# Query weights into freed SBUF, the first head's queries by 128 tokens, the residual kept in SBUF, the last norm in quarters

## The chip, the cores and the metric

The kernel runs on one core of one Trainium2 chip. Each core has TensorE (PE in the profile; its weight loads are PEld), VectorE (DVE), ScalarE (ACT), GpSimd (POOL), the SyncE queue (SP) that only issues transfers here, and 16 DMA engines that all queues share. The metric is the device time of one execution in microseconds, the median over runs.

## The reference, cut to what matters

One layer works on 256 latent tokens and 256 context tokens with 2048 channels. Attention and a gated DeltaNet are computed from a common input projection, merged by gates and projected; the result is added to the stream. Then comes the expert stage, where each token picks 16 experts for each of 8 heads out of 128 x 128:

```python
x = x + g1 * y                                   # residual after the token mixer
hx = modulate(x, norm2_w, sh2, sc2)
q = (hx @ w_q).reshape(t, 8, 2, 128)             # two query halves for each head
s = einsum('thpd,pkd->thpk', q, sub_keys)        # 128 scores for each half
top_s, top_i = top_k(s, 16)                      # best 16 of each half, then the best 16 of 16x16 sums
idx = ...                                        # 128 expert rows for each token (8 heads x 16)
act = gelu(einsum('td,thkd->thk', hx, u[idx]))
x = x + g2 * einsum('thk,thkd->td', softmax(best_s) * act, v[idx])
return rmsnorm(x, final_norm_w)
```

`u` and `v` are tables of 16384 rows of 2048 fp32 numbers. 256 tokens with 128 experts each need 32768 rows of either table, 8 KB a row.

## The kernel before

Everything up to the output projection takes some 1190 us of the span. The output projection is a loop over 16 blocks of 128 channels (line 1190). Each block takes two loads of 512 KB of `wout`, rounded and split by ScalarE and VectorE into two parts for TensorE (`unit`, `split`, `mm3`), and two loads of 512 KB of `wmod` that VectorE reduces (`mod_unit`). The merged branches `mg_hi` and `mg_lo` (pool `mgp`, 32 KB a partition together) are the other operand. The updated residual `xl` has channels on the partitions; `keep_x1` (line 1179) transposes it by 128x128 blocks on TensorE, copies four blocks at a time out of PSUM, and stores them to DRAM (`x1_d`) on ScalarE's queue. After the loop, VectorE scales the 16 blocks of `mg` by the norm, and ScalarE adds the shift and writes `hx`, block by block (lines 1219 to 1221).

The expert stage handles the 256 tokens as two halves t of 128 (a token is a partition). `query(h)` (line 1447) forms the two query halves of a head, each as 16 products over a weight tile of 128x2048 (`wq`, 1 MiB) with 256 tokens as columns, copies them to SBUF and calls `scores`. A product in fp32 is two instructions in the trace. `route` is the ranking of one half of the tokens for one head: a row of small operations on VectorE that ends in 16 columns of row numbers. `first` gathers 128 rows of `u` with one column (GpSimd issues an indirect DMA of 1 MiB) and VectorE multiplies them with the token's `hx` and sums up, in one instruction. `hx_tokens` makes that `hx`, 16 transposes into PSUM. `second` gathers four times 128 rows of `v` and TensorE sums them up, in 32-token groups, with weights in `zw` into PSUM (`y`, four banks). Rows of 8 KB a partition, for weights and gathers alike, come from one pool of 14 buffers (`row()`); a request waits until its buffer is free.

The work is ordered by the planner of the language from the program's order and its estimates; `keep["on"]` and `keep_dve["on"]` fix the program's order on TensorE and VectorE from where they are set. Before, TensorE's order is fixed only from line 1489 on, VectorE's from line 1445. The order of the program is: the queries of head 0, its ranking for the first half, then for heads 1 to 4 the queries and the 16 gathers with the indices of the head before, with pieces of the next ranking between them; queries of heads 5 to 7; then four rounds of 16 steps, each with four gathers of `u` for the round after and four of `v`. Query weights 0 and 1 have tiles of their own (`wqa`), whose memory later becomes `zw`; 2 and 3 are asked for before head 0's queries, the others when their head comes up. `finish` adds the result to the residual and normalizes: the first half between the gathers of the third round, the second half after everything. It loads residual and norm weight through SP into rows.

## Time and profile before

| | |
|---|---|
| median of three runs | 2582.02 us (2573.47 to 2586.72) |
| the profiled execution's own time | 2578.54 us |
| its span, first to last instruction | 2576.8 us |
| granted TensorE clock, mean | 0.826 |
| busy: PE, DVE, ACT, POOL | 69%, 61%, 27%, 35% of the span |
| moved from and to HBM | 803.14 MB, 312 GB/s over the span |
| moved by the gathers' queue | 541.44 MB |

The durations below are from the one profiled execution. Times are counted from the span's start. A share of 1.00 in a DMA column says that all 16 engines were busy throughout. The share of a busy engine over the whole span mixes stages; here the expert stage, from 1190 us on, is looked at by itself.

### The profile page before, as it was taken

To read this page: it belongs to the slowest core of one execution; us is meant where nothing else is said; L and a number is where in the kernel's file an instruction comes from. 1 tells how busy PE (TensorE), PEld (TensorE's weight loads), DVE (VectorE), ACT (ScalarE), POOL (GpSimd) and SP (SyncE) were. 2 spreads that over 40 slices of the span, in tenths; PEclk is the share of its full clock that TensorE was granted. 3 is DMA by queue.
4 is the path that set the end of the run, shared out by engine and by line. 5 is a ranking of instruction groups with operands and counts; after the bars stand their busy time and mean duration, and the time that the engine had idled before them with its cause. 6 is when DMAs were issued, how large, how long until landed. Compare 5 with 4: busy or idle time off the path is not lost.

```text
span 2576.8 us, 28269 instructions
## 1 busy us (share of the span) xinstructions
PE 1774.1 (69%) x9908; PEld 1120.1 (43%) x9908; DVE 1580.3 (61%) x2769; ACT 696.4 (27%) x1627; POOL 890.0 (35%) x1108
## 2 busy tenths in 40 slices
PE   5899889888988999898343744554545445444664
PEld 2568777788888877788333500010000000000110
DVE  5237877778776588885898676656664454444001
ACT  3237656566655554343000100000000010000000
POOL 0000574747576000211423333333333333333331
PEclk7889999999999999999767876676776666766887
DMA  7755443455465588894999999999999999999995
GB/s 292 257 198 177 133 145 124 138 165 162 141 205 191 187 300 264 296 312 147 399 422 422 421 422 421 421 422 421 421 422 421 422 422 422 421 421 422 421 421 230
DMA packets 168526, 803.14 MB, mean 312 GB/s; under 512 B 26400, under 2 KB 45856, under 8 KB 99776
## 3 DMA queue, kind: packets, MB, share of 16 engines
q0 software_dynamic: 75296, 541.44, 50.7%
q1 hardware_dynamic: 76848, 250.58, 28.9%
q10 hardware_dynamic: 16240, 9.32, 1.2%
q8 instruction: 78, 1.28, 0.2%
q14 instruction: 64, 0.52, 0.1%
HBM read 788.94 MB, written 12.33 MB: 311 GB/s over the span
## 4 chain that ended last, share of the span: by engine, by line
DMA 44%; DVE 3%; PE 3%; issue 3%; POOL 1%; ACT 0%; POOLq 0%; ACTq 0%; DVEq 0%
DMA row<-in_u,ix 27%; DMA row<-in_v,ixT 17%; DVE row L181 2%; PE ps_mm L192 2%; POOL row L1257 1%; PE ps_y L192 0%; DVE sml L181 0%; PE ps_g L192 0%; DVE eq L181 0%; ACT row L1410 0%; DMA x_d<-xs 0%; DVE cf L181 0%; DVE bs L181 0%; PE ps_g L197 0%; PE ps_o L192 0%
## 5 line engine op out<-in xcount | busy, mean ns | idle before, releaser
L192 PE MATMUL ps_y<-row,zw 128*32 128x512 f32 x2048 | 572.6, 787 | 515.2 <-DMA row<-in_v,ixT 490.8
L181 DVE SCALAR_TENSOR_TENSOR row<-row,ps_h 128x2048 f32<-128x2048 f32 x256 | 582.1, 2281 | 427.1 <-DMA row<-in_u,ix 402.8
L192 PEld LDWEIGHTS ps_y<-row,zw 128*32 128x32 f32 x2048 | 98.1, 134 | 988.5 <-DMA row<-in_v,ixT 782.5
L1257 POOL DMA_INDIRECT row<-in_u,ix x256 | 240.6, 940 | 419.1 <-DMA row<-in_u,ix 256.3
L1257 POOL DMA_INDIRECT row<-in_v,ixT x256 | 241.2, 942 | 415.1 <-DMA row<-in_v,ixT 345.2
L181 DVE TENSOR_TENSOR lo<-raw,hi 128x512 fp32r<-128x512 f32 x408 | 303.9, 761 | 76.5 <-ACT hi L259 73.2
L192 PE MATMUL ps_mm<-h_hi,hi 128*128 128x256 f32 (+1 forms) x1040 | 342.1, 329 | 10.8 <-DVE gst L181 10.8
L192 PE MATMUL ps_mm<-h_hi,lo 128*128 128x256 f32 (+1 forms) x1040 | 323.4, 311 | 9.2 <-DVE lo L181 9.2
L192 PE MATMUL ps_mm<-h_lo,hi 128*128 128x256 f32 (+1 forms) x1040 | 323.4, 311 | 0.0
L259 ACT CAST hi<-raw 128x512 fp32r<-128x512 f32 x408 | 245.2, 618 | 196.1 <-PE ps_mm L192 123.3
L192 PEld LDWEIGHTS ps_mm<-h_hi,hi 128*128 128x128 f32 x1040 | 204.7, 197 | 31.8 <-DVE gst L181 11.8
L192 PEld LDWEIGHTS ps_mm<-h_hi,lo 128*128 128x128 f32 x1040 | 203.9, 196 | 20.0 <-DVE lo L181 10.3
L192 PEld LDWEIGHTS ps_mm<-h_lo,hi 128*128 128x128 f32 x1040 | 204.7, 197 | 9.3 <-issue 1.2
L821 POOL TENSOR_TENSOR qs<-qs,tq 32x30 f32<-32x30 f32 (+14 forms) x240 | 172.6, 719 | 18.7
L819 POOL TENSOR_TENSOR tq<-qs 32x30 f32<-32x30 f32 (+14 forms) x240 | 168.7, 703 | 18.1
L192 PE MATMUL ps_mm<-hx,row 128*128 128x256 f32 x448 | 108.4, 405 | 96.3 <-DMA row<-in_wq 96.3
L192 PEld LDWEIGHTS ps_mm<-hx,row 128*128 128x128 f32 x448 | 90.9, 205 | 110.6 <-DMA row<-in_wq 97.2
L1381 ACT ACTIVATE a<-a 128x64 f32<-128x64 f32 x4 | 1.0, 256 | 500.9 <-DVE row L181 500.9
L181 DVE TENSOR_TENSOR row<-ps_y,g2r 128x512 f32<-128x512 f32 x8 | 5.2, 678 | 176.0 <-PE ps_y L192 176.0
L1364 ACT ACTIVATE bs<-bs 128x64 f32<-128x64 f32 x4 | 1.0, 256 | 413.6 <-DVE bs L181 413.6
L181 DVE SCALAR_TENSOR_TENSOR mraw<-mraw,crow 128x1024 f32<-128x1024 f32 x73 | 92.9, 1275 | 16.9 <-DMA mraw<-in_wmod 16.5
L181 DVE SCALAR_TENSOR_TENSOR raw<-raw,crow 128x1024 f32<-128x1024 f32 x55 | 72.7, 1322 | 49.2 <-DMA raw<-in_wmod 49.1
(363 smaller groups left out, 2864.2 us busy)
## 6 DMA issues: line engine op xcount, KB each, us to landing
raw<-in_win SPq DMA_DIRECT2D x130, 512.0 KB, 4.4
raw<-in_wmod SPq DMA_DIRECT2D x119, 512.0 KB, 4.8
mraw<-in_wmod SPq DMA_DIRECT2D x73, 512.0 KB, 5.1
raw<-in_wout SPq DMA_DIRECT2D x32, 512.0 KB, 6.3
row<-in_wq SPq DMA_DIRECT2D x14, 1024.0 KB, 13.5
raw<-in_wbb SPq DMA_DIRECT2D x16, 512.0 KB, 5.8
raw<-in_wba SPq DMA_DIRECT2D x16, 512.0 KB, 4.6
wraw<-in_win SPq DMA_DIRECT2D x48, 128.0 KB, 4.8
```

Of the source, the lines that this page charges most:

```text
L181: ins = f(*a, **k)
L192: ins = nc.tensor.matmul(*a, **k)
L259: act.copy(hi, raw)
L819: pool.tensor_tensor(t, m[:, 0:s, s:s + 1].to_broadcast([32, s, w]), m[:, s:s + 1, s + 1:32].to_broadcast([32, s, w]), op=OP.mult)
L821: pool.tensor_tensor(m[:, 0:s, s + 1:32], m[:, 0:s, s + 1:32], t, op=OP.add)
L1257: pool.indirect_dma_start(out=r, out_offset=None, in_=I[table], in_offset=bass.IndirectOffsetOnAxis(ap=ix, axis=0))
L1364: act.activation(bs, bs, AF.Exp)
L1381: act.activation(a, a, AF.Gelu)
```

## The change

The pool of 14 rows becomes two pools of 4 and 9 rows. The 4 lie where `mg_hi` and `mg_lo` were; `row()` takes rows from the two pools in the order 4, 9, 4, 9. Query weights 0 to 3 are asked for into the 4 as soon as that memory is free, 4 to 7 when the larger pool opens, and 8 to 15 one after every eighth gather of heads 1 to 4. The queries of head 0 are formed for tokens 0 to 127 first, with their scores, then come the transposes of `hx_tokens`, then tokens 128 to 255; TensorE's order is fixed from there. The residual is copied from PSUM into an SBUF tile `x1s` and stays there (three blocks at the end of the loop, the last one by itself). The norm weight comes with the column constants and is spread over the partitions by 16 transposes, as the gate `g2r` is. `zw` has memory of its own. `y` is four tiles of one bank each. In `finish`, the product with the norm weight goes to a row of its own (`res`), so it does not overwrite the sum that ScalarE squares; the last scaling and the store go by quarters (0, 3, 1, 2; quarter 3 on ScalarE), and one small root operation is placed in the last round ahead of `finish`.

```diff
-    x1_d = dram.tile([2, 128, D], F32, name="x1_d")
...
     hx = hxp.tile([128, KB, T], F32, name="hx")
+    x1s = hxp.tile([128, 2, D], F32, name="x1s")
...
-    def keep_x1(i):
+    def keep_x1(i, n):
         for t in range(2):
             p = d_ps()
-            for j in range(4):
+            for j in range(n):
                 pe.transpose(p[:, j * 128:(j + 1) * 128], xl[:, i + j, t * 128:(t + 1) * 128], ident)
-            xs = b1.tile([128, 512], F32, name="xs", bufs=2)
-            act.copy(xs, p)
-            act.dma_start(x1_d[t, :, i * 128:(i + 4) * 128], xs)
-    ahead = []
+            act.copy(x1s[:, t, i * 128:(i + n) * 128], p[:, :n * 128])
...
         if i % 4 == 0 and i > 0:
-            keep_x1(i - 4)
-        if i in (11, 13):
-            w = hxp.tile([128, D], F32, name="wqa", tag="wz", bufs=2)
-            sp.dma_start(w, I["wq"][len(ahead)])
-            ahead.append(w)
+            keep_x1(i - 4, 4)
+        if i == 15:
+            keep_x1(12, 3)
...
-    keep_x1(12)
+    keep_x1(15, 1)
     dbg("hx", hx)
     st_mg.close()
+    rp, st_rp = open_pool("rp", side=R)
+    ROWS_R, ROWS_L = 4, 9
+    rows = {"n": 0}
+    def row():
+        i = rows["n"] % (ROWS_R + ROWS_L)
+        rows["n"] += 1
+        p, n = (rp, ROWS_R) if i < ROWS_R else (ex, ROWS_L)
+        return p.tile([128, D], F32, name="row", bufs=n)
+    def wq_load(i):
+        r = row()
+        sp.dma_start(r, I["wq"][i])
+        return r
+    ahead = [wq_load(i) for i in range(4)]
...
-    ROWS = 14
-    def row():
-        return ex.tile([128, D], F32, name="row", bufs=ROWS)
...
-    ahead += [wq_load(i) for i in range(2, 4)]
+    loaded = {"n": 8}
+    ahead += [wq_load(i) for i in range(4, 8)]
...
+    fwr = ex.tile([128, D], F32, name="fwr")
+    zw = [ex.tile([128, 4, 512], F32, name="zw%d" % i) for i in range(2)]
+    for z in zw:
+        pool.memset(z, 0.0)
...
+    def scores(h, q, t, p):
+        for hf in range(2):
+            pe.matmul(p[:, t * T + hf * 128:t * T + (hf + 1) * 128], q[hf][:, t * 128:(t + 1) * 128],
+                      subk[:, hf], start=True, stop=True)
+        if t == 0 and h < 4:
+            s = ex.tile([128, T], F32, name="s", bufs=2)
+        else:
+            s = sc[:, h - 4 if t == 0 else 4 + h]
+        act.copy(s, p[:, t * T:(t + 1) * T])
+        return s
...
-                pe.matmul(y[32 * g:32 * g + 32, cs], zw[f][:, g, 32 * b:32 * b + 32], rows[g][:, cs],
+                pe.matmul(y[c][32 * g:32 * g + 32, :], zw[f][:, g, 32 * b:32 * b + 32], rows[g][:, cs],
...
-        tmp, x, fw = row(), row(), row()
-        sp.dma_start(x, x1_d[t])
-        sp.dma_start(fw, I["fnw"].to_broadcast([128, D]))
+        tmp, res = row(), row()
+        x = x1s[:, t]
         f = fs[:, t]
         cs = [slice(c * 512, (c + 1) * 512) for c in range(4)]
         if t == 0:
-            for c in cs:
-                dve.tensor_tensor(tmp[:, c], y[:, c], g2r[:, c], op=OP.mult)
+            for i, c in enumerate(cs):
+                dve.tensor_tensor(tmp[:, c], y[i], g2r[:, c], op=OP.mult)
             yield
         for i, c in enumerate(cs):
             if t == 1:
-                dve.tensor_tensor(tmp[:, c], y[:, c], g2r[:, c], op=OP.mult)
+                dve.tensor_tensor(tmp[:, c], y[i], g2r[:, c], op=OP.mult)
             dve.tensor_tensor(x[:, c], x[:, c], tmp[:, c], op=OP.add)
             act.activation(tmp[:, c], x[:, c], AF.Square, accum_out=f[:, i:i + 1])
-            dve.tensor_tensor(x[:, c], x[:, c], fw[:, c], op=OP.mult)
+            dve.tensor_tensor(res[:, c], x[:, c], fwr[:, c], op=OP.mult)
             yield
         dve.tensor_reduce(f[:, 4:5], f[:, 0:4], axis=AX.X, op=OP.add)
         dve.tensor_scalar(f[:, 4:5], f[:, 4:5], 1.0 / D, EPS, op0=OP.mult, op1=OP.add)
...
         dve.tensor_scalar(f[:, 7:8], f[:, 7:8], -0.5, 1.5, op0=OP.mult, op1=OP.add)
         dve.tensor_tensor(f[:, 6:7], f[:, 6:7], f[:, 7:8], op=OP.mult)
         yield
-        for c in range(2):
-            xs = x[:, c * 1024:(c + 1) * 1024]
-            if c == 0:
-                act.activation(xs, xs, AF.Copy, scale=f[:, 6:7])
+        for i in (0, 3, 1, 2):
+            if i == 3:
+                act.activation(res[:, cs[i]], res[:, cs[i]], AF.Copy, scale=f[:, 6:7])
             else:
-                dve.tensor_scalar(xs, xs, f[:, 6:7], None, op0=OP.mult)
-            sp.dma_start(out[t * 128:(t + 1) * 128, c * 1024:(c + 1) * 1024], xs)
+                dve.tensor_scalar(res[:, cs[i]], res[:, cs[i]], f[:, 6:7], None, op0=OP.mult)
+            sp.dma_start(out[t * 128:(t + 1) * 128, cs[i]], res[:, cs[i]])
...
+    def query(h, parts):
+        ws = [ahead.pop(0) for _ in range(2)]
+        os_ = [psm("mm") for _ in range(2)]
+        q = [ex.tile([128, T], F32, name="q", bufs=4) for _ in range(2)]
+        p = psm("g")
+        for a, z in parts:
+            for j in range(2):
+                for k in range(KB):
+                    pe.matmul(os_[j][:, a:z], ws[j][:, k * 128:(k + 1) * 128], hx[:, k, a:z],
+                              start=k == 0, stop=k == KB - 1)
+                act.copy(q[j][:, a:z], os_[j][:, a:z])
+            for t in range(a // 128, z // 128):
+                S[h, t] = scores(h, q, t, p)
+            if a == 0 and z == 128:
+                yield
+    def first_queries():
+        g = query(0, ((0, 128), (128, 256)))
+        next(g)
+        o = hx_tokens(0)
+        all_of(g)
+        return o
+    S = {}
+    keep["on"] = True
+    h_ = first_queries()
+    all_of(route(0, 0, S[0, 0]))
     for h in range(1, NH):
-        query(h)
+        all_of(query(h, ((0, 256),)))
         if h < 5:
-            work.append(route(0, h, S[h][0]))
+            work.append(route(0, h, S[h, 0]))
             for c in range(h * 16 - 16, h * 16):
                 first(0, c, h_)
                 if c % 16 > 2:
                     piece()
+                if c % 8 == 7:
+                    ahead.append(wq_load(loaded["n"]))
+                    loaded["n"] += 1
...
-        if h == 2:
-            zw = [hxp.tile([128, D], F32, name="zw%d" % i, tag="wz", bufs=2).rearrange("p (g c) -> p g c", g=4)
-                  for i in range(2)]
-            for z in zw:
-                pool.memset(z, 0.0)
-    for i in range(0, 16, 4):
-        p = psm("g")
-        for j in range(4):
-            pe.transpose(p[:, j * 128:(j + 1) * 128], modc[:, 80 + i + j:81 + i + j].to_broadcast([128, 128]), ident)
-        act.copy(g2r[:, i * 128:(i + 4) * 128], p)
+    for dst, src in ((g2r, modc[:, 80:96]), (fwr, cols[:, C_FN:C_FN + 16])):
+        for i in range(0, 16, 4):
+            p = psm("g")
+            for j in range(4):
+                pe.transpose(p[:, j * 128:(j + 1) * 128], src[:, i + j:i + j + 1].to_broadcast([128, 128]), ident)
+            act.copy(dst[:, i * 128:(i + 4) * 128], p)
...
-        return psy.tile([128, D], F32, name="ps_y", tag="y", bufs=1)
+        return [psy.tile([128, 512], F32, name="ps_y%d" % c, tag="y%d" % c, bufs=1) for c in range(4)]
...
+            if n == 3 and b == 1:
+                tc.keep_in_program_order(act.activation(fs[:, 1, 5:6], epsc, AF.Sqrt))
```

## Rows read from the trace of the kernel before

**Rows 1.** Windows: PE, PEld, DVE, ACT, POOL busy us, clock, DMA share, GB/s.
```profile
1232.00:1420.00 188.00, 69.30 (x280) 58.08 (x280) 174.55 (x269) 9.41 (x31) 60.56 (x66) 0.69 1.01 422
1420.00:2540.00 1120.00, 598.19 (x2172) 128.87 (x2172) 540.90 (x806) 43.71 (x151) 415.69 (x442) 0.72 1.01 421
```

**Rows 2.** Chain that ended last, one link of the long stretch: start, us.
```profile
2266.33 19.13 DMA row<-in_v,ixT
2285.49 0.72 issue
```

**Rows 3.** Windows between the last projection weights and the first gather.
```profile
1184.00:1192.00 8.00, 7.96 (x66) 7.55 (x64) 1.62 (x3) 1.32 (x3) 0.00 (x0) 1.00 0.01 2
...
1215.00:1220.00 5.00, 5.00 (x29) 4.51 (x28) 4.62 (x21) 0.36 (x1) 0.00 (x0) 1.00 0.01 3
```

**Rows 4.** DMA issues with KB and median us to landing; line 1263's landings.
```profile
row<-in_wq SPq DMA_DIRECT2D x14, 1024.0 KB, 13.5
...
row<-x_d SPq DMA_DIRECT2D x2, 1024.0 KB, 8.9
...
DMA to landing us min/median/max: 5.3/13.5/21.8
```

**Rows 5.** Timeline of SP's queue: start, us from first to last issue.
```profile
1203.19 188.47 SPq L1263 DMA_DIRECT2D row<-in_wq  x14
...
1238.51 2.82 SPq L1263 DMA_DIRECT2D row<-in_wq  x2
...
2522.24 0.33 SPq L1398 DMA_DIRECT2D row<-x_d  x1
```

**Rows 6.** Timeline of VectorE: the last product of the output projection is used.
```profile
1191.56 0.48 DVE L181 SCALAR_TENSOR_TENSOR xl<-ps_mm,modc,xl 128x256 f32<-128x256 f32 x1 [5.73 <-PE ps_mm L192]
```

**Rows 7.** Timelines and chain (PE) from hx to the first gathered row.
```profile
1196.62 6.50 ACT L1221 ACTIVATE hx<-mg,modc 128x256 f32<-128x256 f32 x16 [1.95 <-DMA x_d<-xs]
...
1197.18 15.65 PE ps_mm L192 x64
...
1214.28 0.29 DVE L181 MAX8 sml<-s 128x8 f32<-128x128 f32 x1 [12.66 <-ACT s L1291]
...
1223.76 0.17 DVE L181 CAST ix<-ef 128x16 uint32<-128x16 f32 x1
...
1224.89 1.02 POOL L1257 DMA_INDIRECT row<-in_u,ix  x1 [10.19 <-DVE ix L181]
...
1231.02 2.29 DVE L181 SCALAR_TENSOR_TENSOR row<-row,ps_h 128x2048 f32<-128x2048 f32 x1 [7.09 <-DMA row<-in_u,ix]
```

**Rows 8.** Timeline of TensorE: transposes of 128 columns, and the next product.
```profile
1214.79 1.15 PE L197 MATMUL ps_h<-ck,hx 128*128 128x128 f32 x9
1215.77 6.42 PE L192 MATMUL ps_mm<-hx,row 128*128 128x256 f32 x29
```

**Rows 9.** VectorE's groups by form, 1225 to 1422 us: busy, mean ns, idle before.
```profile
L181 DVE SCALAR_TENSOR_TENSOR row<-row,ps_h 128x2048 f32<-128x2048 f32 x65 | 146.4, 2279 | 18.2 <-DMA row<-in_u,ix 17.7 <-issue 0.3
```

**Rows 10.** Waits of TensorE, 1085 to 1192 us: total, times, longest.
```profile
PE ps_mm L192 <- ACT hi L259: 5.6, 6, 1.7
```

**Rows 11.** Timelines of PE, DVE, ACT and SP after the last row; issues.
```profile
2552.43 5.12 PE L192 MATMUL ps_y<-row,zw 128*32 128x512 f32 x26 [1.43 <-DMA row<-in_v,ixT]
...
2557.59 0.69 DVE L181 TENSOR_TENSOR row<-ps_y,g2r 128x512 f32<-128x512 f32 x1 [175.98 <-PE ps_y L192]
...
2559.84 0.69 DVE L181 TENSOR_TENSOR row<-row 128x512 f32<-128x512 f32 x1 [0.84 <-ACT row L1410]
...
2568.24 1.28 ACT L1415 ACT_TABLE_LOAD   x1
...
2570.74 1.15 ACT L1425 ACTIVATE row<-row,fs 128x1024 f32<-128x1024 f32 x1 [1.00 <-DVE fs L181]
...
2571.52 0.81 SPq L1428 DMA_DIRECT2D out<-row  x2
...
out<-row SPq DMA_DIRECT2D x2, 512.0 KB, 3.1
```

More of the change, by code (lines that the diff above doesn't have):

```diff
@@ L30 @@
 CHUNKS = tuple((k, k + 2) for k in range(0, 16, 2))
-C_BMOD, C_N1, C_N2, C_QN, C_KVN, C_CONV, C_DNW, C_ALOG, C_DTB = 0, 96, 112, 128, 132, 134, 254, 255, 256
-N_COL = 257
+C_BMOD, C_N1, C_N2, C_QN, C_KVN, C_CONV, C_DNW, C_ALOG, C_DTB, C_FN = 0, 96, 112, 128, 132, 134, 254, 255, 256, 257
+N_COL = 273
 K_ID, K_IOTA, K_I16, K_PERSIST = 0, 128, 256, 272
@@ L140, in layout @@
     cols[64:80, C_DTB] = dn_dt_bias[0].reshape(16)
+    cols[:, C_FN:C_FN + 16] = final_norm_w.reshape(16, 128).T
     a["cols"] = cols
@@ L162, in layout @@
     a["v"] = np.ascontiguousarray(peer_v[0])
-    a["fnw"] = np.ascontiguousarray(final_norm_w.reshape(1, D))
     a["ck"], a["ca"] = shape_constants()
@@ L1259, in gather @@
         return r
-    def wq_load(i):
-        r = row()
-        sp.dma_start(r, I["wq"][i])
-        return r
-    ahead += [wq_load(i) for i in range(2, 4)]
+    loaded = {"n": 8}
+    ahead += [wq_load(i) for i in range(4, 8)]
     subk = ex.tile([128, 2, 128], F32, name="subk")
@@ L1278, in tile_block @@
                     (("bs", F32), ("ef", F32), ("ix", U32), ("ixT", U32), ("a", F32))})
-    def scores(h, q):
-        p = psm("g")
-        out_ = []
-        for t in range(2):
-            for hf in range(2):
-                pe.matmul(p[:, t * T + hf * 128:t * T + (hf + 1) * 128], q[hf][:, t * 128:(t + 1) * 128],
-                          subk[:, hf], start=True, stop=True)
-            if t == 0 and h < 4:
-                s = ex.tile([128, T], F32, name="s", bufs=2)
-            else:
-                s = sc[:, h - 4 if t == 0 else 4 + h]
-            act.copy(s, p[:, t * T:(t + 1) * T])
-            out_.append(s)
-        return out_
+    def scores(h, q, t, p):
[8 more added lines that the diff above has]
+        return s
     def route(t, h, s):
@@ L1441, in all_of @@
             pass
-    S = []
     keep_dve["on"] = True
-    def query(h):
-        qs = []
-        for j in range(2):
-            o = psm("mm")
-            w = ahead.pop(0) if ahead else wq_load(2 * h + j)
-            for k in range(KB):
-                pe.matmul(o[:, :T], w[:, k * 128:(k + 1) * 128], hx[:, k], start=k == 0, stop=k == KB - 1)
-            q = ex.tile([128, T], F32, name="q", bufs=4)
-            act.copy(q, o[:, :T])
-            qs.append(q)
-        S.append(scores(h, qs))
-    query(0)
-    all_of(route(0, 0, S[0][0]))
-    h_ = hx_tokens(0)
+    def query(h, parts):
[23 more added lines that the diff above has]
+    all_of(route(0, 0, S[0, 0]))
     for h in range(1, NH):
-        query(h)
+        all_of(query(h, ((0, 256),)))
         if h < 5:
-            work.append(route(0, h, S[h][0]))
+            work.append(route(0, h, S[h, 0]))
             for c in range(h * 16 - 16, h * 16):
@@ L1469, in tile_block @@
                     piece()
+                if c % 8 == 7:
+                    ahead.append(wq_load(loaded["n"]))
+                    loaded["n"] += 1
             while work:
                 piece()
-        if h == 2:
-            zw = [hxp.tile([128, D], F32, name="zw%d" % i, tag="wz", bufs=2).rearrange("p (g c) -> p g c", g=4)
-                  for i in range(2)]
-            for z in zw:
-                pool.memset(z, 0.0)
-    for i in range(0, 16, 4):
-        p = psm("g")
-        for j in range(4):
-            pe.transpose(p[:, j * 128:(j + 1) * 128], modc[:, 80 + i + j:81 + i + j].to_broadcast([128, 128]), ident)
-        act.copy(g2r[:, i * 128:(i + 4) * 128], p)
+    for dst, src in ((g2r, modc[:, 80:96]), (fwr, cols[:, C_FN:C_FN + 16])):
[4 more added lines that the diff above has]
+            act.copy(dst[:, i * 128:(i + 4) * 128], p)
     st_psb.close()
@@ L1485, in y_tile @@
     def y_tile():
-        return psy.tile([128, D], F32, name="ps_y", tag="y", bufs=1)
-    keep["on"] = True
+        return [psy.tile([128, 512], F32, name="ps_y%d" % c, tag="y%d" % c, bufs=1) for c in range(4)]
     y = [y_tile(), None]
@@ L1493, in tile_block @@
         if n == 0:
-            work += [route(0, h, S[h][0]) for h in range(5, 8)] + [route(1, h, S[h][1]) for h in range(4)]
+            work += [route(0, h, S[h, 0]) for h in range(5, 8)] + [route(1, h, S[h, 1]) for h in range(4)]
         if n == 1:
-            work += [route(1, h, S[h][1]) for h in range(4, 8)]
+            work += [route(1, h, S[h, 1]) for h in range(4, 8)]
         for b in range(16):
@@ L1518, in tile_block @@
     st_ex.close()
+    st_rp.close()
     st_hx.close()
```

## Prediction

> **What bounds the kernel now.** I read the windows first, then the chain of waits, then the queue's own views. From 1232 us to 2540 us of the span the 16 DMA engines are busy to a share of 1.01 at 421 to 422 GB/s, while TensorE, ScalarE and GpSimd are well under full throughout, and VectorE in all but the first 188 us [rows 1]. The chain says the same: a gather of 1 MiB waits 19.13 us for its data, 0.72 us pass, and the next link follows [rows 2]. A 1 MiB transfer at 421 GB/s takes 1.0486 MB / 421 GB/s = 2.49 us, so 19.85 us is eight transfers: eight gathers are in flight, and the queue stays full. In this stage only three things count: how many MiB pass, when the stream starts, and what follows its last byte. In those first 188 us VectorE is nearly as full (174.55 us busy) [rows 1]; this matters below.
>
> Around the stream are two idle places. Before it, between the last output-projection weights and the first gather, the engines are at 0.01 (1184 to 1192 us) and again at 0.01 (1215 to 1220 us) [rows 3]. After it, the last row wakes TensorE at 2552.43 us and the span ends at 2576.8 us: 24.4 us in which little more than two output stores moves.
>
> **Bytes that leave the stream.** Fourteen loads of query weights (1024 KB each), two reloads of the residual and, by the same pattern, two of the norm weight pass through SP's queue [rows 4]. The first two of the fourteen leave at 1203.19 us; the third and fourth only at 1238.51 us [rows 5], and the other ten later still, so 12 lie in the full stretch. The residual and norm loads lie there too; the second pair leaves at 2522.24 us, among the last gathers [rows 5]. That is 16 MiB beside 512 gathers. After the change four loads (0 to 3) go into the memory of the merged branches, free when the last output-projection product is done, about 1191.5 us [rows 6], and four (4 to 7) when the scaled residual is no longer read, about 1203 us. The quickest of these loads landed 5.3 us after its issue [rows 4]; with 2.49 us for each further one the first four land by 1191.5 + 5.3 + 3 x 2.49 = 1204.3 us and the next four by 1216 us: both inside the valley of [rows 3]. Loads 8 to 15 stay in the stream; the other four vanish. So 16 - 8 = 8 transfers, 8 x 2.49 = **19.9 us**.
>
> The rule of the Trainium skill that bears on this is in "DMA: Bandwidth & Descriptors", section "Issuing engines are not separate DMA queues": transfers from all issuing engines run on the same 16 engines and interleave. By it a load asked for earlier wins nothing where the engines are full; the trace agrees with the premise, as gathers and weight loads together never pass 422 GB/s [rows 1]. This is the third rival below.
>
> **The stream starts earlier.** Now the first head's products take 15.65 us for 64 instructions of 256 columns, 0.245 us each, and then VectorE ranks from 1214.28 us and the first gather leaves at 1224.89 us, 10.6 us behind [rows 7]. With 128 columns the first product (32 instructions) is paced by ScalarE, which delivers the 16 blocks of hx in 6.50 us from 1196.62 us [rows 7], so it ends near 1203.3 us. The second takes 32 x 0.122 = 3.9 us if half the columns cost half: 1207.2 us instead of 1212.8 us. Gain 5.6 us; first gather at 1219.3 us. No row shows this product at 128 columns. The nearest do: nine 128x128 instructions, each with a weight load of its own, start at 1214.79 us, and the next product at 1215.77 us, 0.109 us each [rows 8]. Bounds: 0 us gained (128 columns cost as much as 256) and 5.6 us; I take the latter. The first load must be there by 1199.4 us (1203.3 less 3.9); it lands at 1191.5 + 5.3 = 1196.8 us. If the four loads share the engines and land together at 1204.3 us, 7.8 us of products start only then, and all but 0.7 us of the gain is gone.
>
> The Trainium skill, "TensorE: Matmul & The Clock Gate", section "Back-to-back issue gap", speaks against halving: it gives about 81 ns per product at 128 columns and 131 ns at 512, so a quarter of the columns costs 0.62. An estimate on that line has half of 256 columns at about 0.83; the second product would take 6.5 us and the sum would be 2.6 us smaller. The 0.109 us of [rows 8] go by columns, so the sum does too.
>
> **What the other parts cost.** The second half of the first head (7.8 us) and sixteen transposes (16 x 0.109 = 1.7 us [rows 8]) now stand between the first scores and the second head on TensorE. The second head's scores come about 5 us later than now (1236 instead of 1231 us), and VectorE, in program order, needs them after four rows: about 1 us of waiting, which the queued gathers cover. Rows: 14 become 13, and at the start 8 of the 13 hold weights. Five gathers go at once, four of the held rows come free as the first two heads' products end, to about 1235 us, and used rows come back from 1228 us on. I followed row by row who frees what, with the durations above and VectorE's 2.28 us a row [rows 9]: the first 16 gathers and two weight loads keep the engines full to about 1267 us, the next head's indices are there near 1261 us, and the queue runs dry for about 1.5 us near 1403 us and some 3 us where the first half's last norm holds two rows. Against the 5.6 us I set **5 us** lost; bounds 0 and the 14 us of the second rival. VectorE's own work for the first 64 rows is 146.4 us (65 of them) [rows 9] and four rankings at the 9.65 us that the first one takes (1214.28 to 1223.93 us) [rows 7], 185 us in all: from the first row in use at 1225.4 us to 1410 us. The 64 gathers and 8 weight loads need 72 x 2.49 = 179 us from 1223 us, to 1402 us, and eight gathers in flight bridge the 8 us between the two, so neither holds the other up.
>
> Keeping the residual in SBUF replaces a store by nothing: the copies out of PSUM stay. Filling the norm weight's tile costs 16 more transposes (16 x 0.109 us) and four copies out of PSUM behind the last queries, some 4 us beside a full DMA queue, which covers it: nothing. If that cover is gone, 4 us.
>
> **Before the stream** six residual stores of 128x512 elements (1.5 MiB) and one weight load leave the output-projection stage. TensorE waits there 5.6 us for weights that ScalarE rounds as they land [rows 10]; the 5.6 us are the most that fewer bytes can give back, and nothing the least. I take **3 us**, the middle.
>
> **After the last row.** Now 5.12 us of products end, then VectorE starts (2557.59 us), and in each quarter the multiplication by the norm weight waits 0.84 us for ScalarE's square, because it overwrites what the square reads [rows 11]. Four quarters last to 2568.24 us, where a table load of 1.28 us lies in the way of the root; the halves are scaled from 2570.74 us (1.15 us) and stored from 2571.52 us, 0.4 us an issue and 3.1 us a store, the last landed near 2575.0 us [rows 11]. After: each quarter has its own PSUM tile, so the first starts when 2 of the 26 products are done, 0.6 us behind the last row. VectorE then needs 3 x 0.69 = 2.07 us a quarter without the wait, 8.3 us: TensorE's 5.12 us run beneath, and the last square is done at about 9.1 us. From there to the scale it is 2.5 us now (2568.24 to 2570.74); without the table load, but with some 0.6 us of summing that ran beneath it, 1.8 us: 10.9 us. The first quarter is scaled by 11.3 us; four stores issued 0.4 us apart end at 12.5 us, the last lands at 15.2 us if half the bytes take a little less than 3.1 us, and 1.8 us remain to the end of the span as now: 17.0 us instead of 24.4 us, **7.4 us**. If a quarter is stored as slowly as a half, 7.0 us; if twice as fast, 8.2 us.
>
> **Sum**: 19.9 + 5.6 - 5 + 3 + 7.4 = 30.9 us. The profiled execution took 2578.5 us (span 2576.8 us), 3.5 us under the median of the three runs, so 2547.6 us on its footing and **2551 us** as a median. What a measurement can tell from no change is about 0.5%, 12.9 us.
>
> **Rivals.** (1) *Some row count decides, slower.* With 13 rows instead of 14 the gathers may wait for rows in the long stream, not only at its start. A gather alone takes 1231.02 - 1224.89 = 6.1 us from issue to use [rows 7], 2.5 transfers; only with two or fewer in flight do the engines idle, 6.1 / 2 - 2.49 = 0.57 us a gather. 55 such gathers eat the 31 us, all 512 would cost 290 us. Against it: eight are in flight [rows 2], so 13 rows leave 5 for use before the queue even thins. A case of a hundred such gathers gives 2607 us. (2) *Rows in strict turn.* If the ninth gather must have the row of weight load 4, it waits for the third head's first product, and three more wait for the next ones, 7.8 us apart where the engines need 2.49 us. That idles them about 17 us, of which 14 are lost: 17 us gained, 2565 us. Nothing in the rows shows which row a gather gets. (3) *The early loads do not land in the valley*, or VectorE holds the first stage and the weights' share of the bytes is not given back: then only the four residual and norm loads count, 10 us less, 21 us gained, 2561 us. For it: VectorE's 174.55 of 188 us [rows 1]. (4) *Not told from no change*: both (2) and (3), 30.9 - 14 - 10 = 7 us gained, 2575 us.
>
> **Chances.** Forecast 0.62 (2543 to 2559 us, by the 0 to 5.6 us of the start, 0 to 5.6 us of the stage before and 3 us for rows), rival 2 0.13, rival 3 0.13, rival 4 0.08, rival 1 0.04. The range 2541 to 2567 us holds the forecast, most of rivals 2 and 3, and no more than 2 in 10 is left out. Faster by over 0.5% is below 2569 us: the first three but a little, 0.86; within 0.5% 0.10; slower 0.04.
>
> **What would show it.** Right: four weight loads leaving near 1191.5 us and four near 1203 us; the first gather near 1219 us; no residual or norm load in the stream; a full DMA share from about 1223 us and the last row some 20 us earlier than 2552.4 us less what the earlier stage gives; VectorE's last quarter about 8 us behind the last row. Wrong: DMA share under 0.95 between 1240 and 1280 us with GpSimd waiting for a query product (rival 2); ranking that begins where it does now; fewer than eight gathers in flight in the long stretch (rival 1). What would make the number wrong most easily is a first weight load later than 1199 us, or a planner's order of the copies on ScalarE that holds up the query products.

## The result, and the profile after

| | before | after |
|---|---|---|
| median of four executions | 2580.75 us | 2540.32 us |
| lowest and highest | 2573.47, 2586.72 us | 2534.12, 2543.52 us |
| span of the profiled execution | 2576.8 us | 2541.8 us |
| ratio after / before | | 0.9842, 95% interval 0.9809 to 0.9875 |

The changed kernel is 1.6% faster, 40.4 us by the medians. The prediction said 2551 us within 2541 to 2567 us: the time lies 0.7 us below that range. Three of the five terms came out near their size and one on the good side of it; the cost set against them was too small, and one term was missing.

Windows of the stream after (columns as in [rows 1], which they answer):

```profile
1232.00:1420.00 188.00, 114.45 (x458) 95.26 (x456) 177.34 (x278) 15.55 (x47) 62.85 (x67) 0.77 0.99 414
1420.00:2060.00 640.00, 319.89 (x1066) 56.39 (x1066) 389.28 (x655) 30.55 (x112) 245.80 (x259) 0.71 1.01 427
2060.00:2110.00 50.00, 23.59 (x68) 4.12 (x72) 25.43 (x34) 6.38 (x12) 13.76 (x15) 0.62 0.81 322
2110.00:2500.00 390.00, 220.41 (x861) 40.53 (x854) 119.84 (x106) 5.19 (x19) 150.29 (x160) 0.76 1.01 427
```

Two things here were not forecast. The long stretches run at 427 GB/s at the same DMA share of 1.01 where [rows 1] had 421. And there is a hole at 2060 to 2110 us, with a smaller one in the first 188 us.

The start after, timelines of SP, ScalarE, TensorE, VectorE and GpSimd ([rows 5, 7]):

```profile
1191.37 2.09 SPq L1232 DMA_DIRECT2D row<-in_wq  x4
1203.12 1.99 SPq L1232 DMA_DIRECT2D row<-in_wq  x4
1196.56 6.49 ACT L1216 ACTIVATE hx<-mg,modc 128x256 f32<-128x256 f32 x16 [1.95 <-DVE mg L181]
1197.12 10.04 PE L192 MATMUL ps_mm<-hx,row 128*128 128x128 f32 x64 [3.47 <-ACT hx L1216]
1209.01 0.68 PE L192 MATMUL ps_g<-subk,q 128*128 128x128 f32 x4 [1.84 <-DMA subk<-in_subk]
1211.27 7.31 PE L192 MATMUL ps_mm<-hx,row 128*128 128x128 f32 x64
1210.54 0.30 DVE L181 MAX8 sml<-s 128x8 f32<-128x128 f32 x1 [8.98 <-ACT s L1295]
1220.48 1.02 POOL L1264 DMA_INDIRECT row<-in_u,ix  x1 [13.76 <-DVE ix L181]
```

Both groups of weight loads leave when forecast. The first products are done at 1207.2 us, as forecast, and 64 instructions of 128 columns take 7.31 us (0.114 us each; [rows 7] had 0.245 us at 256). But the scores then wait for `subk`, the sub-keys. Their load is asked for only at 1203.08 us, with the second four weight loads, when the memory of its tile is free; it takes 5.5 us to land.

The tail after, timelines of TensorE, VectorE, ScalarE and SP, and one line of DMA issues ([rows 11]):

```profile
2524.21 3.62 PE L192 MATMUL ps_y<-row,zw 128*32 128x512 f32 x26 [1.41 <-DMA row<-in_v,ixT]
2525.30 0.69 DVE L181 TENSOR_TENSOR row<-ps_y,g2r 128x512 f32<-128x512 f32 x1 [164.88 <-PE ps_y L192]
2526.75 0.69 DVE L181 TENSOR_TENSOR row<-x1s,fwr 128x512 f32<-128x512 f32 x1
2532.91 0.63 ACT L1412 ACTIVATE row<-x1s 128x512 f32<-128x512 f32 x1 [1.33 <-DVE x1s L181]
2534.11 0.20 ACT L1417 ACTIVATE fs<-fs 128x1 f32<-128x1 f32 x1 [0.47 <-DVE fs L181]
2535.31 1.28 DVE L181 TENSOR_SCALAR row<-row,fs 128x512 f32<-128x512 f32 x3
2535.82 1.80 SPq L1429 DMA_DIRECT2D out<-row  x4
out<-row SPq DMA_DIRECT2D x8, 256.0 KB, 3.3
```

VectorE starts 1.1 us behind the last row, the product with the norm weight waits for nothing, and no table load stands before the root: 17.6 us from the last row to the end instead of 24.4 us.

### The profile page after: what moved, and what is told of

Read it like the earlier page. It is cut to its first block, busy times and chain, and to the rows that moved or that the text cites. A ratio compares the mean times of both kernels' runs of the same rounds, so it can differ in the third digit from the quotient of the medians.

```text
span 2541.8 us, 28426 instructions
## 1 busy us (share of the span) xinstructions
PE 1788.7 (70%) x9988; PEld 1132.7 (45%) x9988; DVE 1581.1 (62%) x2773; ACT 699.6 (28%) x1636; POOL 901.2 (35%) x1108
## 4 chain that ended last, share of the span: by engine, by line
DMA 54%; PE 20%; DVE 8%; issue 7%; POOL 6%; ACT 4%; another core or an unknown queue 0%; SPq 0%; DVEq 0%; ACTq 0%; POOLq 0%
DMA row<-in_v,ixT 39%; PE ps_mm L192 12%; PE ps_d L192 4%; DMA row<-in_u,ix 3%; DMA raw<-in_wout 3%; POOL qs L820 3%; POOL tq L818 2%; PE ps_r L192 2%; DMA raw<-in_wmod 2%; DVE lo L181 2%; DMA wraw<-in_win 1%; DVE row L181 1%; DMA mraw<-in_wmod 1%; ACT hi L259 1%; POOL row L1264 1%
## 5 line engine op out<-in xcount | busy, mean ns | idle before, releaser
L820 POOL TENSOR_TENSOR qs<-qs,tq 32x30 f32<-32x30 f32 (+14 forms) x240 | 182.3, 760 | 18.7
L192 PE MATMUL ps_mm<-hx,row 128*128 128x256 f32 (+1 forms) x576 | 130.2, 391 | 48.4 <-DMA row<-in_wq 44.9
L192 PEld LDWEIGHTS ps_mm<-hx,row 128*128 128x128 f32 x576 | 111.0, 212 | 66.0 <-DMA row<-in_wq 46.6
```

Source lines behind the costliest of these rows:

```text
L192: ins = nc.tensor.matmul(*a, **k)
L820: pool.tensor_tensor(m[:, 0:s, s + 1:32], m[:, 0:s, s + 1:32], t, op=OP.add)
```

## The experiments

Medians scatter with what comes before the queries' input `hx`, which few of the edits below touch: it ended anywhere from 1181 to 1206 us of the span. So each profiled execution is also read from the first instruction that writes `hx` on. After and the runs e13 and e14 have the same code from there and took 1345.2, 1340.4 and 1345.7 us, so differences of less than 5 us say little. The ratios are to executions of before that were taken beside each run (medians 2581.8 to 2582.3 us). The three columns behind `hx` starts are stretches that follow one another and add up to the last column.

| run | median us (executions) | ratio to before, 95% | `hx` starts | from there to the first gather | first gather to last row | last row to end | `hx` to end |
|---|---|---|---|---|---|---|---|
| before | 2580.75 (4) | 1 | 1196.6 | 28.3 | 1327.5 | 24.4 | 1380.2 |
| after | 2540.32 (4) | 0.9842 (0.9809 to 0.9875) | 1196.6 | 23.9 | 1303.7 | 17.6 | 1345.2 |
| e1 | 2566.33 (6) | 0.9929 (0.9902 to 0.9957) | 1206.0 | 28.2 | 1309.2 | 22.8 | 1360.2 |
| e2 | 2551.64 (6) | 0.9883 (0.9854 to 0.9911) | 1180.8 | 24.5 | 1316.8 | 18.0 | 1359.2 |
| e3 | 2531.76 (6) | 0.9801 (0.9777 to 0.9826) | 1193.1 | 24.1 | 1298.9 | 17.6 | 1340.6 |
| e4 | 2523.63 (6) | 0.9779 (0.975 to 0.9808) | 1183.8 | 24.3 | 1293.5 | 18.3 | 1336.0 |
| e5 | 2516.54 (5) | 0.9739 (0.9715 to 0.9763) | 1192.9 | 21.9 | 1290.1 | 17.6 | 1329.6 |
| e6 | 2523.3 (5) | 0.9767 (0.9746 to 0.9787) | 1194.6 | 21.9 | 1292.4 | 17.6 | 1331.9 |
| e7 | 2590.36 (10) | 1.0033 (1.0018 to 1.0048) | 1194.5 | 40.1 | 1327.2 | 24.4 | 1391.8 |
| e8 | 2543.35 (6) | 0.9846 (0.982 to 0.9872) | 1188.3 | 24.4 | 1312.1 | 18.4 | 1354.9 |
| e9 | 2537.95 (1) | | 1187.4 | 21.9 | 1309.3 | 17.5 | 1348.7 |
| e10 | 2538.47 (1) | | 1187.0 | 22.2 | 1309.1 | 18.4 | 1349.7 |
| e11 | 2526.08 (4) | 0.9778 (0.9755 to 0.9801) | 1189.1 | 28.9 | 1289.7 | 17.6 | 1336.2 |
| e12 | 2535.76 (5) | 0.9821 (0.9795 to 0.9848) | 1192.0 | 21.9 | 1301.6 | 17.5 | 1341.1 |
| e13 | 2538.74 (1) | | 1196.6 | 23.5 | 1298.6 | 18.4 | 1340.4 |
| e14 | 2534.54 (1) | | 1187.1 | 25.6 | 1301.9 | 18.2 | 1345.7 |

**Where the row buffers begin (e1, e2, e3, e9, e10).** The change holds the norm weight in 16 more columns of `cols`, the second tile on the left side of SBUF: 64 bytes per partition, which shift everything behind it. By the program's layout all 14 row buffers of before begin 192 bytes past a multiple of 256; of after's 13, the nine left ones begin on a multiple, the four right ones 224 past. The traces hold no addresses; they show which shifts are fast.

```diff
# e1, on before
-N_COL = 257
+N_COL = 273
# e2, on after: ahead of the left row buffers
+    ex.tile([128, 48], F32, name="pad")
# e3, on after: behind x1s, on the right side
+    hxp.tile([128, 56], F32, name="pad")
# e9, on e5 (e10: 88 and 16 in place of 72 and 32)
-    hxp.tile([128, 40], F32, name="pad")
+    hxp.tile([128, 72], F32, name="pad")
+    ex.tile([128, 32], F32, name="padl")
```

> Theory A: the stream's rate hangs on where a row buffer begins in SBUF. In the kernel before, all 14 buffers begin 192 bytes past a multiple of 256; the 64 bytes per partition that the change adds to cols put the nine left ones of the kernel after on multiples of 256. Here the kernel before gets those 64 bytes and nothing else, so that all 14 are on multiples of 256: the stream 1420:2040 goes from 421 to 428 to 432 GB/s and the time falls by 18 to 30 us. Theory B: the faster stream of the kernel after comes from what it no longer does in it (8 MiB of plain loads, two residual reads), or it is a matter of the run: 421 GB/s, time within 5 us of before.

> The kernel after with 192 unused bytes ahead of its nine left row buffers, so that they begin 192 bytes past a multiple of 256 as in the kernel before; the four right ones stay at 224. Theory A: 421 GB/s in 1420:2040 as before, time up by 15 to 18 us on the kernel after (2555 to 2559). Theory B: 427 GB/s, 2540 as the kernel after.

> The kernel after with 224 unused bytes on the right side, so that the four right row buffers also begin on multiples of 256. Theory A: these four are still slow in the kernel after (its gathers come 2.44 and 2.49 us apart in groups), so 427 goes to 429 to 431 GB/s and the time falls by 5 to 10 us (2530 to 2535). Theory B: 427 GB/s, 2540.

> The version with all three changes (e5), its 13 row buffers moved to 128 bytes past a multiple of 256. A gather starts every 2.447 us where all buffers are on multiples of 256 (e1, e3), every 2.485 at 192 and 224 (before, e2). If 128 bytes are the unit, 2.447 again; if it is 256, 2.47 to 2.49 and some 19 us more in the stream.

> The same with the row buffers 64 bytes past a multiple of 256. If 64 bytes are the unit, the 192 of the kernel before would have been as fast as 0, which e1 and e2 speak against: 2.47 to 2.49 us a gather. If the cost grows with the distance from the multiple, the pitch lies between 2.447 and 2.485, nearer to the first.

The same window of e1, e2, e3, e9 and e10, in this order (columns as before):

```profile
1500.00:1800.00 300.00, 149.23 (x499) 26.79 (x500) 191.54 (x360) 13.23 (x53) 115.68 (x122) 0.69 1.01 427
```
```profile
1500.00:1800.00 300.00, 146.91 (x496) 26.59 (x496) 190.39 (x353) 13.23 (x53) 112.06 (x120) 0.71 1.01 421
```
```profile
1500.00:1800.00 300.00, 149.31 (x516) 27.84 (x512) 192.88 (x357) 13.24 (x53) 115.91 (x122) 0.72 1.01 427
```
```profile
1500.00:1800.00 300.00, 144.77 (x486) 26.12 (x490) 190.78 (x357) 13.23 (x53) 112.60 (x120) 0.71 1.01 421
```
```profile
1500.00:1800.00 300.00, 150.97 (x495) 27.46 (x496) 190.86 (x355) 13.23 (x53) 112.66 (x120) 0.69 1.01 421
```

The DMA engines are busy to 1.01 in all five; only the rate differs, and it goes with the address alone. Theory A holds, though the 428 to 432 GB/s forecast for e1 and the 429 to 431 for e3 were not reached: both have after's 427. Over 1450 to 1940 us, the mean of the regular steps (2.3 to 2.7 us) from the start of one gather to the start of the next is 2.448 us in e1, 2.447 in e3 and 2.448 in e5 (all buffers on multiples of 256), 2.484 in before, 2.486 in e2, 2.485 in e9 and 2.484 in e10, and 2.454 in after, where some four steps of 2.49 us and nine of 2.42 to 2.47 follow one another in turn. Of the four places 64 bytes apart that were tried, one is fast, and 64, 128 and 192 bytes past it cost the same 1.5%: the unit is 256 bytes, or a multiple of it. From `hx` to the end e1 gains 20.0 us, e2 loses 14.0, e9 loses 19.1 on e5. e1's and e2's medians move by 16 and 11 us, a little under the forecasts; e3's forecast holds by its median (8.6 us) and by the time between gathers (2.447 against 2.454 us, 3.6 us over 520 transfers); its 4.6 us from `hx` on are under what single executions can tell.

The rule that fits is in the Trainium skill, "DMA: Bandwidth & Descriptors", section "How a descriptor splits into AXI transactions": a read that does not begin on a multiple of 256 bytes has its first piece begin at the boundary below, and the bytes fetched in vain cost 32-byte beats. The runs agree with 256 as the unit, though here the shifted side is the one that is written. They do not agree that the cost grows with the distance: an estimate on the page's count for 8 KB would be 0.8, 1.6 and 2.3% at 64, 128 and 192 bytes.

**The first half's norm (e4).** `finish(0)` takes two of the 13 rows for a few tens of us while gathers need them. GpSimd's timeline in after, and a window:

```profile
2078.21 0.94 POOL L1264 DMA_INDIRECT row<-in_v,ixT  x1 [17.81 <-ACT row L1412]
2089.31 0.94 POOL L1264 DMA_INDIRECT row<-in_u,ix  x1 [7.67 <-PE ps_y L192]
2117.56 0.94 POOL L1264 DMA_INDIRECT row<-in_v,ixT  x1 [14.67 <-DMA out<-row]
```
```profile
2070.00:2080.00 10.00, 5.41 (x6) 0.54 (x6) 7.80 (x10) 3.45 (x7) 1.49 (x2) 0.59 0.32 124
```

A gather stands 17.8 us for the norm's square (line 1412) and another 14.7 us for its output store, and every gather behind them in GpSimd's order stands too. The count of rows alone does not do this: in before, the same step holds three of 14 rows, which leaves 11 as here, and the stream stays at 1.01 [rows 1]. One thing that differs is that `row()` now hands out two pools, of four and nine, in a fixed turn; that was not tried by itself.

```diff
-        tmp, res = row(), row()
         x = x1s[:, t]
+        tmp, res = (sc[:, 0:8].rearrange("p a b -> p (a b)"), x) if t == 0 else (row(), row())
```

> The kernel after with the first half's norm working in the score tile (dead by then) and in the residual's own tile instead of two of the 13 rows. If the two rows make the dip of the DMA share at 2060 to 2100, the waits of GpSimd for <-ACT row and <-DMA out<-row go, the share stays over 0.95 and the time falls by 7 to 11 us (2529 to 2533). Rival: the dip comes from TensorE, which waits for VectorE to empty the first half's sums before the second half's rows are multiplied (<-PE ps_y at 2046 and 2089): the dip stays, with at most 3 us gained.

```profile
2060.00:2110.00 50.00, 27.05 (x84) 4.39 (x88) 24.63 (x31) 4.30 (x7) 18.04 (x19) 0.68 1.01 425
```

In e4's window the hole is gone; the rival fell. By the windows the hole costs 50 x (1 - 322/427) = 12.3 us. The time won is less: from first gather to last row e4 takes 10.2 us less than after and 5.1 and 8.4 us less than e13 and e14, whose code there is after's; e9 and e10, which also keep the norm out of the rows, take 7.5 and 7.7 us less than e2 at the same rate. That is some 8 us. The medians' 16.7 us are more than forecast; the spread ahead of `hx` blurs them. The last section has a reading of the difference between the hole and the time won.

**Everything together (e5), and a 14th row (e6).**

```diff
# e5, on after: e4's line and, behind x1s,
+    hxp.tile([128, 40], F32, name="pad")
+    subk = hxp.tile([128, 2, 128], F32, name="subk")
+    act.dma_start(subk, I["subk"])
+    iota16 = hxp.tile([128, 16], F32, name="iota16")
+    act.dma_start(iota16, I["ck"][:, K_I16:K_I16 + 16])
...
-    subk = ex.tile([128, 2, 128], F32, name="subk")
-    act.dma_start(subk, I["subk"])
-    iota16 = ex.tile([128, 16], F32, name="iota16")
-    act.dma_start(iota16, I["ck"][:, K_I16:K_I16 + 16])
# e6, on e5
-    ROWS_R, ROWS_L = 4, 9
+    ROWS_R, ROWS_L = 4, 10
-        q = [ex.tile([128, T], F32, name="q", bufs=4) for _ in range(2)]
+        q = [ex.tile([128, T], F32, name="q", bufs=2) for _ in range(2)]
```

> The kernel after with all 13 row buffers on multiples of 256 bytes, the first half's norm in the score tile, and the sub-keys and the index row loaded before the output projection instead of behind the eight query weights. From the run-free part (from the start of the queries' input to the end: 1345.2 us in the kernel after) come off 4 to 5 for the right buffers, 9 to 12 for the norm and 2 for the sub-keys: 1327 to 1330 us, median 2518 to 2524. If the sub-keys' load is not what the first scores wait for, the first gather stays 29 us behind the last output-projection sum (28 to 26.5 if it is).

> As the run before it, with a 14th row buffer (room from two of the four query tiles). If the short supply of rows makes the waits of GpSimd for TensorE's and VectorE's use of rows at 1235 to 1300 (some 4 us of DMA time lost in the kernel after), one row more takes off 1 to 4 us; if they come from VectorE's ranking of the first heads, nothing changes (within 1 us from the queries' input to the end).

TensorE and GpSimd in e5:

```profile
1203.33 1.01 PE L192 MATMUL ps_g<-subk,q 128*128 128x128 f32 x4
1214.78 1.02 POOL L1269 DMA_INDIRECT row<-in_u,ix  x1 [11.73 <-DVE ix L181]
```

The scores no longer wait, and the first gather comes 21.9 us after `hx` instead of 23.9. That the load was late for being behind the weights is not so: it landed 5.5 us after its issue in after, 5.9 in e8 with three weight loads fewer beside it, and 5.7 in e1 with two in all. It was asked for late. e5 takes 1329.6 us from `hx` to the end, as forecast, and 2516.5 us in all, 1.5 us below the forecast; it is faster than both kernels, 2.6% under before. One row more changes nothing that can be told (+2.3 us). As e5 has no thin place in the first stage (425 GB/s over 1232 to 1310 us), this says that 13 rows do there, not what thinned the stream in after.

**Loads ahead (e7, e8, e12).**

```diff
# e7, on before
-        if i in (11, 13):
-            w = hxp.tile([128, D], F32, name="wqa", tag="wz", bufs=2)
-            sp.dma_start(w, I["wq"][len(ahead)])
-            ahead.append(w)
...
-    ahead += [wq_load(i) for i in range(2, 4)]
+    ahead += [wq_load(i) for i in range(0, 4)]
# e8, on after (with 48 columns of pad that keep the left rows on 256); e12, on e5
-    loaded = {"n": 8}
-    ahead += [wq_load(i) for i in range(4, 8)]
+    loaded = {"n": 4}
...
+        while len(ahead) < 2:
+            ahead.append(wq_load(loaded["n"]))
+            loaded["n"] += 1
```

> The kernel before without the two query-weight loads inside the output projection; they are requested after it with the next two. If these 2 MiB are what the projection lost (105 us from its first to its last sum in the kernel before, 98 in the kernel after), it takes 98 to 100 us here, and the stream starts 3 to 8 us later after it, since the first queries now wait for weights. If it was the copies and residual writes on ScalarE, the projection stays at 103 to 105.

> The kernel after, but query weights 4 to 7 are not requested ahead into freed memory: the stream carries 12 of them as in the kernel before instead of 8. By the sum of the prediction that puts 4 x 2.45 = 9.8 us back into the stream: median 2550 (2547 to 2556). If the loads ahead were worth nothing because the stream's early part is not bound by transfers, 2538 to 2543.

> The version with all three changes (e5), with query weights 4 to 7 requested in the stream as in e8. There the median rose by 3 us on the kernel after, while the profiled execution from the start of the queries' input to the end rose by 9.7. If each load in the stream costs its 2.45 us, that part goes from 1329.6 to 1339 to 1341 here, and the median from 2516.5 to 2524 to 2529. If the rows that the loads ahead hold cost half of it back in the first 80 us, 1333 to 1335 and 2519 to 2523.

Four loads on demand cost 9.7 us (e8) and 11.5 us (e12) from `hx` to the end. That this is four times 2.45 us is chance. The first of the four leaves at 1194.9 us in e8 and 1198.6 us in e12, before the first gather, so only three go back into the stream, 7.3 us. The rest is a hole where GpSimd waits for the products of the later heads (e8; e12 has the like over 1432 to 1446 us at 259 GB/s):

```profile
1431.00:1447.00 16.00, 14.42 (x83) 10.95 (x85) 7.71 (x15) 6.88 (x13) 6.55 (x7) 1.00 0.69 249
1431.75 0.93 POOL L1265 DMA_INDIRECT row<-in_v,ixT  x1 [13.82 <-PE ps_mm L192]
```

It costs 5 to 7 us in both, and e8 lacks a hole of 4 to 5 us that after has at 1274 to 1286 us (below). The medians, +3.0 and +19.2 us, lie one under and one over the forecasts; e8's alone would have spoken for the other theory.

What a transfer in the stream is worth shows between e1 and e5. All their buffers are on multiples of 256, neither has a hole, and e5 moves 8 MiB less from first gather to last row (windows of these stretches, e1, then e5):

```profile
1234.26:2543.44 1309.18, 678.49 (x2518) 195.19 (x2516) 715.98 (x1074) 53.96 (x184) 484.33 (x512) 0.73 1.01 424
1214.78:2504.88 1290.10, 690.43 (x2572) 205.84 (x2570) 716.11 (x1076) 57.98 (x191) 483.51 (x512) 0.75 1.01 424
```

At the same 424 GB/s that is 19.1 us, 2.4 us each. Before against e9 and e10, at the slower rate, gives 18.2 and 18.4 us.

In e7 the first gather leaves 40.1 us after `hx` instead of 28.3, more than forecast, and the kernel is 8.6 us slower than before: loads early enough for the first head count. The projection's first to last sum, before and e7:

```profile
L181 DVE SCALAR_TENSOR_TENSOR xl<-ps_mm,modc,xl x16: 477/484/485, 1086.3 to 1191.6; 128x256 f32<-128x256 f32 x16
L181 DVE SCALAR_TENSOR_TENSOR xl<-ps_mm,modc,xl x16: 475/483/486, 1085.9 to 1189.4; 128x256 f32<-128x256 f32 x16
```

103.5 us without the weight loads, 102.6 in e1 with them, 105.3 in before: they are not what the stage loses.

**The residual's writes (e13, e14).** Both runs are after with the residual written to DRAM again; nothing reads it.

```diff
             act.copy(x1s[:, t, i * 128:(i + n) * 128], p[:, :n * 128])
+            act.dma_start(x1_d[t, :, i * 128:(i + n) * 128], x1s[:, t, i * 128:(i + n) * 128])
# e14: sp.dma_start
```

> The kernel after, which also writes the residual to DRAM from ScalarE's queue as the kernel before does (nothing reads it). In the kernel before the 5th, 9th and 13th step of the output projection, in which the residual is copied and written, take 8.2, 7.9 and 7.3 us, in the kernel after 6.9, 6.4 and 5.7, and e7 excluded the weight loads. If the writes on ScalarE's queue are the difference, the three steps take 7.9 to 9 us, 7.5 to 9 and 6.5 to 7.5, and the stage 102 to 104 instead of 98.5. If the order of the copies is (the change moved them), 6.9, 6.4 and 5.7 stay.

> The same with the writes issued from SyncE's queue. If it is the issuing on ScalarE (0.8 us on its queue for two writes), the steps stay at 6.9, 6.4 and 5.7. If it is the transfer, or the weight loads that are queued behind a write which waits for its copy, they take 1 us more each, or longer than in e13.

The same line of after, e13 and e14:

```profile
L181 DVE SCALAR_TENSOR_TENSOR xl<-ps_mm,modc,xl x16: 477/483/485, 1092.9 to 1191.4; 128x256 f32<-128x256 f32 x16
```
```profile
L181 DVE SCALAR_TENSOR_TENSOR xl<-ps_mm,modc,xl x16: 475/484/486, 1087.0 to 1191.5; 128x256 f32<-128x256 f32 x16
```
```profile
L181 DVE SCALAR_TENSOR_TENSOR xl<-ps_mm,modc,xl x16: 476/484/485, 1072.3 to 1181.9; 128x256 f32<-128x256 f32 x16
```

98.5, 104.5 (102 to 104 were forecast) and 109.6 us. In e13 the 5th, 9th and 13th step take 8.3, 9.1 and 6.9 us, in after 6.9, 6.4 and 5.7: the writes are what the stage lost. The other executions bear it out: in the eleven without the writes the three steps take 6.3 to 7.2, 6.3 to 6.7 and 5.2 to 5.8 us, in the four with writes from ScalarE (before, e1, e7, e13) 7.8 to 8.3, 7.9 to 9.4 and 6.9 to 7.3. The whole stage scatters more, 96.6 to 102.0 us (mean 99.2) against 102.6 to 105.3 (mean 103.9), so the writes are worth some 5 us. On SyncE's queue they cost more (11.0, 10.0 and 5.5 us), with 4.8 us of waiting there for the copies ahead of weight loads. How the 5 us divide between issuing and transfer stays open.

**The first head by 256 columns (e11).**

```diff
-        g = query(0, ((0, 128), (128, 256)))
-        next(g)
-        o = hx_tokens(0)
+        g = query(0, ((0, 256),))
         all_of(g)
+        o = hx_tokens(0)
```

> The version with all three changes (e5), with the first head's queries multiplied by 256 tokens at once as in the kernel before. By the sum of the prediction the first half's 128 tokens bring the first gather 5.6 us nearer: it goes from 21.9 us after the start of the queries' input to 27 to 28, and the time up by 5 to 6 us (2521 to 2523). If the scores wait for other things anyway, 22 to 24 us.

TensorE and GpSimd in e11:

```profile
1189.67 16.93 PE L192 MATMUL ps_mm<-hx,row 128*128 128x256 f32 x64 [3.47 <-ACT hx L1221]
1217.99 1.02 POOL L1269 DMA_INDIRECT row<-in_u,ix  x1 [18.73 <-DVE ix L181]
```

The first gather comes 28.9 us after `hx`, 7.0 us later than in e5; the time is 6.6 us longer from `hx` to the end and 9.5 us by the medians. Some 1.3 us of the 7.0 are TensorE's clock in this execution: the same 64 instructions took 15.65 us in before [rows 7], where the granted clock was 0.73 over their first 6 us (1197.18 to 1203.18), against 0.52 here (1189.67 to 1195.67), between its two levels of 1.2 and 2.4 GHz (0.50 and 1.00). TensorE had waited 3.5 us for `hx` in both. So the step is worth about the 5.6 us that the prediction gave it, once nothing else holds the scores.

## Why the prediction was right, and where it failed

| term | predicted us | measured us | from |
|---|---|---|---|
| bytes out of the stream | 19.9 | 18 to 19 | first gather to last row: e1 against e5; before against e9, e10 |
| earlier first gather | 5.6 | 4.4 | 28.3 to 23.9 after `hx` |
| row shortage | -5 | about -8, and -4 to -5 in one execution | e4, e9, e10 for the norm; after's hole at 1274 us |
| projection stage | 3 | about 5 | means 99.2 and 103.9, without and with the residual's writes |
| tail | 7.4 | 6.8 | 24.4 to 17.6 |
| rate of the stream | none | 14 to 16 | e2; 520 MiB x (2.484 - 2.454) |

**The step that failed** is the one that priced every transfer at 2.49 us, before and after, as if the rate of [rows 1] were a constant of the stream. The diff moved the row buffers by 64 bytes per partition, and 9 of 13 became 1.5% faster to fill. This term alone is larger than the miss of 11 us; without it (e2) the median is 2551.6 us, the number predicted. That is luck: from `hx` on e2 gains 21.0 us, where the terms predicted for that part add up to 27.9.

**Row shortage** was right in place and wrong in size. I set some 3 us where the first half's norm holds two rows; it is a hole of 10 to 12 us in the six executions in which the changed kernel holds them so, and some 8 us of time. The row-by-row count took the two rows as gone, not the order: one gather stands for a held row, and those behind it with free rows stand too. The 1.5 us near 1403 us did not show; a hole of about 4 us lies at 1274 to 1286 us of after instead. That is rival 2's mark, GpSimd waiting for a query product:

```profile
1274.00:1280.00 6.00, 6.00 (x30) 5.28 (x29) 4.91 (x7) 0.23 (x1) 0.05 (x1) 1.00 0.55 233
1280.00:1286.00 6.00, 6.00 (x30) 5.28 (x29) 2.38 (x3) 0.14 (x1) 4.66 (x5) 1.00 0.73 258
1279.95 0.94 POOL L1264 DMA_INDIRECT row<-in_u,ix  x1 [13.26 <-PE ps_mm L192]
```

It took 4 to 5 us, not 14, and it belongs to this execution: e13, with the same code from `hx` on, has no such hole (1232 to 1310 us; after: share 0.95, 398 GB/s):

```profile
1232.00:1310.00 78.00, 65.41 (x302) 55.77 (x300) 73.71 (x119) 7.07 (x19) 22.46 (x25) 0.96 1.01 426
```

Why it differs between executions stays open. Rivals 1, 3 and 4 are out: gathers never ran short in the long stretches outside the norm's hole, and the early loads left at 1191.37 and 1203.12 us.

**The start** lost 1.2 us of its 5.6 to a DMA that I had left out although it is issued in the same lines: `subk`, asked for at 1203.08 us and landing 5.5 us later, behind the end of the first products. At half the columns half the time was about right: 0.114 us against the 0.221 us of [rows 8] (29 in 6.42 us; the 0.245 of [rows 7] hold ScalarE's pace and a lower clock as well), so 0.52 of the time and not the 0.83 set against it. The end of the first products at 1207.2 us was right too.

**The projection stage** gained about 5 us, within the bounds of 0 and 5.6 us, where I took 3. The wait that the bound rested on, TensorE's for rounded weights, fell from the 5.6 us of [rows 10] to 1.1 us in after, but it does not go with the stage; the second line is e13, whose stage took 104.5 us:

```profile
PE ps_mm L192 <- ACT hi L259: 1.1, 3, 0.4
PE ps_mm L192 <- ACT hi L259: 2.6, 6, 0.9
```

In e7 it is 2.1 us at a stage of 103.5 us, in e11 3.0 us at 101.5. So a size near the bound was luck: the bound came from a wait that is not what the writes cost. In the pair of profiled executions the gain didn't show, as the stage began 6.6 us later in after; that is one reason why the spans differ by 35.0 us and the medians by 40.4.

**The tail** came out at 17.6 us against 17.0, by the steps given; the stores of both halves take 3.3 us at the median, at the slow end of the bounds.

## What to carry to other kernels

Where a stream is bound by transfers, look at what a diff does to the addresses of its buffers: 16 unused columns in a neighbouring tile were worth 16 to 20 us here (e1). A buffer borrowed from a ring that an in-order queue feeds costs the whole queue for as long as it is held, so scratch belongs in memory that is dead anyway. A small load that the first step needs is asked for early, into memory that is free early: 128 KB took 5.5 us to land.

## What the runs showed of the hardware that was not expected

The 16 DMA engines drift apart in a long gather stream. Windows before the last row, first e5 (last row at 2504.88 us), then the last 4 us of after, e9 and e2:

```profile
2494.88:2498.88 4.00, 3.63 (x28) 1.01 (x28) 0.00 (x0) 0.00 (x0) 0.00 (x0) 1.00 0.86 363
2498.88:2500.88 2.00, 0.88 (x2) 0.14 (x2) 0.00 (x0) 0.00 (x0) 0.00 (x0) 1.00 0.48 201
2500.88:2504.88 4.00, 1.21 (x4) 0.14 (x3) 0.00 (x0) 0.00 (x0) 0.00 (x0) 1.00 0.06 25
```
```profile
2520.21:2524.21 4.00, 1.21 (x3) 0.14 (x2) 0.00 (x0) 0.00 (x0) 0.00 (x0) 1.00 0.68 287
2514.61:2518.61 4.00, 1.17 (x4) 0.14 (x3) 0.00 (x0) 0.00 (x0) 0.00 (x0) 1.00 0.05 23
2518.01:2522.01 4.00, 1.99 (x3) 0.18 (x3) 0.00 (x0) 0.00 (x0) 0.00 (x0) 0.70 0.48 199
```

In e5, whose stream had no hole, the share is down to 0.06, one engine's worth of sixteen, for the last 4 us before the last row is there; in after, with the hole at 2070 us, it is still 0.68. All 16 executions divide so: the six with that hole (after, e2, e3, e8, e13, e14) have 0.42 to 0.68 in their last 4 us, the ten without it 0.05 to 0.10, at either rate of the stream. This fits a hole that lets the slower engines catch up, and why taking out 10 to 12 us of it gives back some 8. Which engines are the slower ones, and why, no row read here says.

And what comes before `hx` took 1181 to 1206 us in 16 profiled executions, and still 1181 to 1197 us in the five (after, e2, e3, e4, e8) whose code is the same there but for unused bytes: a spread as large as most terms of the sum. No row read here says why.
